# A hybrid attention layer on one core: first x block and warm-up, gates of the first up group, and the place of product 6 in the first output task

## The chip, the cores and the metric

The kernel runs on one core of a Trainium2 chip. The metric is the device time of one execution in microseconds (us); lower is better. The engines are PE (TensorE, matrix products), PEld (its weight loads), DVE (VectorE), ACT (ScalarE), POOL (GpSimd) and SP (SyncE); the last two mostly issue transfers (DMA) here.

## The reference

One layer over 512 tokens of width 2048, all in float32:

```
hn    = rmsnorm(x, norm_g)
proj  = hn @ w_in                      # q, k, v, gate of three branches, 4 forget logits, 3 merge gates
ya    = forgetting attention(q, k, v, f_logit)      # branch A, 4 heads of 128
yb    = chunked attention with relative bias        # branch B
yc    = stick-breaking attention                    # branch C
ys    = stack(ya, yb, yc) * silu(gate)
up    = einsum('bsnw,nwd->bsnd', ys, w_up)          # 512 -> 2048 for each branch
merged = sum over branches of sigmoid(merge gate) * up
out   = x + merged @ w_out                          # 2048 -> 2048
```

## The kernel before

**Products in two parts.** Every float32 operand of a large product is split in an upper part and the rest: ACT writes the upper part (`wh` for weights, line 366; `hi` for activations), DVE the lower part (`wl = raw - wh`, line 371; `lo`). Three matmuls (hi by wh, lo by wh, hi by wl) give one product. A weight block ("unit") is 256 rows by 512 columns: two pieces of 128 x 512. There are three `wh` buffers, two `wl` buffers and eight `raw` buffers, so the copies of a block begin when PE has left an older one.

**Order.** The instructions of PE, ACT and DVE stand in an order that a small planner in the kernel writes out: `Flow` keeps a clock per engine, tasks (Python generators) yield events, buffers or an engine with a cost, and the task that can start first is recorded next. The planner's costs and due times set only that order; on the chip each engine takes its list in order and waits by semaphores. Lists of `units` give the order of weight blocks, and `at(u, task)` starts a side task when PE's list comes to unit `u`.

**Stages.** (1) Until about 54 us: x is loaded transposed in 16 blocks of 128 x 512 (`loads`, on SP's queue), scaled by `norm_g` and split (`prep_x`), and multiplied with the columns of branch C's first head (`first_head`); x in its natural layout comes beside it for the norm (`norm_x`). PE begins with `WARM` small matmuls on an identity. (2) Until about 1014 us: the other heads and the merge gates. Behind the first group of gates, the products of 512 tokens by 2048 by two groups of 512 columns are done as Strassen tasks: seven products (named 5, 1, 6, 7, 4, 2, 3 in the order `PLAIN`) over half the tokens, each over four chunks `c` of the inner dimension, in place of eight. A merge gate's rows are stored to DRAM (`spill`). (3) 1014 to 1158 us: the up projection, in groups `g` of 512 output columns and, in each, the branches C, B, A. PE fills four `acc` banks, one for each block of 128 tokens (`tb`), by two units; for each bank DVE multiplies it with the sigmoid of the merge gate (`taken`, line 1251), which frees the bank. The gates are loaded back from DRAM by SP and go through ACT's sigmoid (`gates_of`, lines 1232 to 1236); `at(len(units) - 3 + tb // 2, ...)` starts these tasks. (4) From 1154 us: the output projection, two Strassen tasks (`out_task`). The merged rows of the last up group are turned on PE and combined into Strassen's operands (`m23`, `m2`, `m4`) by `merged_b` on DVE and ACT at the beginning of this stage.

In a Strassen task the weights of product 6 are those of product 5 plus those of product 1 of the same chunk: DVE adds them in the raw buffer (`sum_up`, line 574) once product 5's `wl` is made, and copies follow. The first output task is the one task with an order of its own: products 5, 1 and 6 for the chunks 0 and 1, then for the chunks 2 and 3, then `PLAIN`. So that three products are open at once, its product 6 has two banks of the other pool (`other = (6,)`, `att` in place of `acc`; each pool has four banks).

Of the kernel before, what the change touches and what calls it, by code (L numbers as in the profile page):

```python
# [8 lines left out]
F32 = mybir.dt.float32  # L9
F32R = mybir.dt.float32r  # L10
BF16 = mybir.dt.bfloat16
# [4 lines left out]
P = 128  # L16
S = 512
# [11 lines left out]
HS = S // 2  # L29
EPS = 1e-6  # L30
NEG = -1e30
WARM = 42
SCALE = HD ** -0.5
LA = 2

# [119 lines left out]
def act_us(n, x=1):  # L155
    return x * (0.075 + 0.00095 * n)


def dve_us(n, x=1):
    return x * (0.1 + 0.00105 * n)  # L160
# [3 lines left out]
def hybrid_kernel(  # L164
# [26 lines left out]
    def nm(s):  # L191
        uid[0] += 1
        return f"{s}_{uid[0]}"
# [6 lines left out]
    def t2(s, dt=F32):  # L200
        return tp.tile([P, S], dt, tag="t2", name=nm(s))
# [87 lines left out]

    nc.scalar.preload_act_table_set("natural_log_exp_and_others")  # L290
    small_in = cp.tile([P, consts.shape[1]], F32, name="small_in")
    nc.scalar.dma_start(small_in, consts)
    gn = small_in[:, 0:KT]
    gqk = small_in[:, KT:KT + 4]
    bfc = small_in[:, KT + 4:KT + 5]
    wf = small_in[:, KT + 5:].rearrange("p (k h) -> p k h", h=NH)

    epsc = cp.tile([P, 1], F32, name="epsc")
    nc.gpsimd.memset(epsc, EPS)
    nhepsc = cp.tile([P, 1], F32, name="nhepsc")  # L300
# [38 lines left out]
    def at(u, g, slack=5.0):  # L339
        side.setdefault(u, []).append((g, slack))  # L340
# [20 lines left out]
    def prep(u):  # L361
        n = u.shape[0] * S
        u.hi = wp.tile([P] + u.shape, F32R, tag="wh", name=nm("wh"), bufs=LA + 1)
        yield u.there
        yield ACT, act_us(n)
        nc.scalar.activation(u.hi, u.raw, AF.Copy)  # L366
        set_(u.ready_hi)
        yield wls, 1
        u.lo = wp.tile([P] + u.shape, F32R, tag="wl", name=nm("wl"), bufs=LA)
        yield DVE, dve_us(n)  # L370
        nc.vector.tensor_sub(u.lo, u.raw, f(u.hi))  # L371
        set_(u.ready)
        u.split_done()
# [39 lines left out]
    first_ps = att()  # L413
    atts.free.pop()
    nc.vector.memset(first_ps, 0.0)
    for _ in range(WARM):
        nc.tensor.matmul(first_ps[:, :P], identb, identb, start=True, stop=True)
    xps.free.clear()


# [5 lines left out]
    def prep_x(kt):  # L426

        due = (5.0 + 3.2 * kt,)
        yield x_in[kt]
        x = xraw[kt]  # L430
        if kt < 2:
            g = gn[:, kt:kt + 1]
            yield (ACT, act_us(S), *due)
            nc.scalar.activation(xs[kt].hi, two(x), AF.Copy, scale=g)
            set_(raw_hi[kt])
            yield (DVE, dve_us(S), *due)
            nc.vector.scalar_tensor_tensor(xs[kt].lo, two(x), g, f(xs[kt].hi), op0=ALU.mult, op1=ALU.subtract)
            set_(raw_ev[kt])
            yield (DVE, 0.5, due[0] + 5.0)
            nc.vector.tensor_scalar_mul(x, x, g)  # L440
            set_(scaled[kt])
            return
        if kt < 10:
            yield (DVE, 0.5, *due)
            nc.vector.tensor_scalar_mul(x, x, gn[:, kt:kt + 1])
        else:
            yield (ACT, 0.65, *due)
            nc.scalar.activation(x, x, AF.Copy, scale=gn[:, kt:kt + 1])
        set_(scaled[kt])
        yield from split(xs[kt].hi, xs[kt].lo, two(x), S, raw_ev[kt], due, raw_hi[kt])  # L450
# [777 lines left out]
    def gates_of(n, g, tb):  # L1228
        yield last_head.event("hl", 2)
        yield t2s, 1  # L1230
        t = sig[n, g, tb] = t2("sg")
        yield fetch(t, gl[n, g, tb], flow.now, 256)
        yield last_head.event("g")
        yield ACT, act_us(S) + 0.1
        nc.scalar.activation(t, t, AF.Sigmoid)  # L1235
        set_(sig_ev[n, g, tb])
# [111 lines left out]
    for g in (0, 2, 1, 3):  # L1348
        for b in range(NB):
            for tb in range(QB):  # L1350
                at(len(units) - 3 + tb // 2, lambda n=(C, B, A)[b], g=g, tb=tb: gates_of(n, g, tb))
            units.extend(up_units(g, b))
        for i in range(QB):
            at(len(units) - 1, lambda g=g, i=i: turned_m(g, i))
# [6 lines left out]
    def out_task(i):  # L1361
        where = dict(c11=(0, 0), c12=(2, 0), c21=(0, 1), c22=(2, 1))

        def place(name, tb):
            b, q = where[name]
            return b + tb, 2 * i + q

        def done(name, tb, c):
            yield ACT, 0.05
            nc.scalar.dma_start(out[place(name, tb)[0], place(name, tb)[1]], c)  # L1370
            stored(t2s, 1, 256)

        def rest(name, tb):
            return xn[place(name, tb)[0], place(name, tb)[1]]

        def src(m, half, c):
            return w_out[2 * i + m, CH * half + c]

        order, other = PLAIN, ()
        if i == 0:  # L1380
            order = [(p, c) for cs in ((0, 1), (2, 3)) for p in (5, 1, 6) for c in cs]
            order += PLAIN[3 * CH:]
            other = (6,)
        return Strassen(src, mops, done, order, other, rest).units

    for i in range(2):
# [3 lines left out]
    def loads():  # L1390
        def x(kt):
            yield t2s, 1
            xraw[kt] = t2("x")
            x_in[kt].t = fetch(xraw[kt], xT[kt], 0.0, 256).t

# [30 lines left out]
                spawn(u.after(), 0.0, flow.fin)  # L1426

    line[0] = 0.8
    flow.fin = 5.0
    spawn(loads(), 0.0, 0.0)  # L1430
    for kt in range(KT):
        spawn(prep_x(kt), 5.0)
# [62 lines left out]
```

## Time and profile before

| | |
|---|---|
| median of 3 runs | 1318.59 us (1318.33 to 1319.23) |
| profiled execution | 1318.87 us, span from first to last instruction 1317.2 us |
| busy share of the span | PE 99%, weight load 82%, DVE 78%, ACT 57%, POOL 7% |
| granted TensorE clock | 1.000 |
| transfers | 266.03 MB, 202 GB/s mean |

The span is what the profile's times run over, beginning at 0; the profiled execution's own time is 1.7 us more. Rows of a timeline give start and duration in us, the engine, the line, what is written and read, the number of instructions merged, and in brackets the time the engine was idle before and what released it. SPq, ACTq and POOL rows with DMA are the issue of a transfer, not the transfer.

### The profile page before, as it was taken

Reading aid. Unit: us, or ns where it says so; the run is one execution under the profiler, and the core shown is the slowest. Engines: PE = TensorE matmul, PEld = TensorE weight load, DVE = VectorE, ACT = ScalarE, POOL = GpSimd, SP = SyncE. Lnnn points to the kernel's source line nnn. Section 1 sums busy time; section 2 is a strip of 40 time slices with the busy share of each in tenths; the row PEclk is TensorE's granted clock in tenths of the full one; section 3 lists DMA queues with packets and bytes.
Section 4 is the critical chain, followed back from the end, with each engine's and each line's share of the span. In section 5 each row is a group of like instructions: output and inputs, shape, how many; then the busy total and the mean of one; then the engine's idle time right before and its main releaser. Section 6 shows DMA issues by size and latency. Waiting matters only on the chain.

```text
span 1317.2 us, 17191 instructions
## 1 busy us (share of the span) xinstructions
PE 1306.8 (99%) x6034; PEld 1078.7 (82%) x6034; DVE 1023.2 (78%) x1420; ACT 751.5 (57%) x1271; POOL 91.2 (7%) x115
## 2 busy tenths in 40 slices
PE   9999999999999999999999999999999999999998
PEld 7788888888888888888888888888887788878787
DVE  5877787887878777687776877778789668798667
ACT  7655464564557656566466654667568555454342
POOL 0000001110011100111011110110000000000110
PEclk9999999999999999999999999999999999999999
DMA  9755677866778757777577775777776656648883
GB/s 358 218 139 147 182 209 190 231 176 178 207 196 231 197 166 232 176 225 205 170 226 176 224 208 168 224 176 224 220 250 197 235 192 208 161 97 249 245 240 128
DMA packets 89063, 266.03 MB, mean 202 GB/s; under 512 B 11264, under 2 KB 11264, under 8 KB 88976
## 3 DMA queue, kind: packets, MB, share of 16 engines
q1 hardware_dynamic: 71552, 206.16, 46.5%
q0 software_dynamic: 14976, 54.53, 23.1%
q10 hardware_dynamic: 2448, 4.24, 0.8%
q8 instruction: 47, 0.77, 0.2%
q14 instruction: 40, 0.33, 0.1%
HBM read 245.19 MB, written 19.70 MB: 201 GB/s over the span
## 4 chain that ended last, share of the span: by engine, by line
PE 96%; DMA 2%; DVE 1%; ACT 1%; issue 0%; SPq 0%; ACTq 0%; POOLq 0%; DVEq 0%
PE acc L265 89%; DMA raw<-in_w_out 2%; PE att L801 1%; PE att L926 1%; PE att L260 1%; PE att L261 1%; PE att L262 1%; PE att L1016 1%; PE att L1015 1%; PE att L1285 1%; PE att L1014 1%; PE att L265 1%; ACT sg L1235 0%; DVE wl L371 0%; PE att L1118 0%; DMA x<-in_xT 0%
## 5 line engine op out<-in xcount | busy, mean ns | idle before, releaser
L371 DVE TENSOR_TENSOR wl<-raw,wh 128x1024 fp32r<-128x1024 f32 (+1 forms) x405 | 493.5, 1220 | 208.1 <-PE acc L265 116.1
L366 ACT ACTIVATE wh<-raw 128x1024 fp32r<-128x1024 f32 (+1 forms) x405 | 426.0, 1054 | 365.8 <-PE acc L265 276.3
L265 PE MATMUL acc<-wh,x 128*128 128x512 f32 x1664 | 429.8, 392 | 0.1
L265 PEld LDWEIGHTS acc<-wh,x 128*128 128x128 f32 x1664 | 308.7, 188 | 64.7 <-ACT t L246 0.9
L265 PE MATMUL acc<-wh,t 128*128 128x512 f32 x1056 | 272.6, 391 | 0.0
L265 PE MATMUL acc<-wl,x 128*128 128x512 f32 x832 | 229.8, 390 | 0.0
L265 PEld LDWEIGHTS acc<-wh,t 128*128 128x128 f32 x1056 | 196.7, 188 | 40.2
L265 PEld LDWEIGHTS acc<-wl,x 128*128 128x128 f32 x832 | 155.9, 188 | 33.1 <-DVE wl L371 0.4
L265 PE MATMUL acc<-wl,t 128*128 128x512 f32 x528 | 149.3, 390 | 0.0
L281 POOL DMA_DIRECT2D raw<-in_w_col x88 | 76.0, 864 | 877.5 <-ACT wh L366 195.3
L574 DVE TENSOR_TENSOR raw<-raw,raw 128x1024 f32<-128x1024 f32 x104 | 126.7, 1218 | 0.0
L265 PEld LDWEIGHTS acc<-wl,t 128*128 128x128 f32 x528 | 98.4, 188 | 19.6
L265 PE MATMUL acc<-wh,m 128*128 128x512 f32 x416 | 105.1, 390 | 1.9 <-ACT wh L366 1.9
L265 PE MATMUL acc<-wh,y 128*128 128x512 f32 x384 | 103.7, 391 | 1.3 <-DVE sg L1251 1.3
L265 PEld LDWEIGHTS acc<-wh,m 128*128 128x128 f32 x416 | 77.9, 188 | 18.8 <-ACT wh L366 2.7
L265 PEld LDWEIGHTS acc<-wh,y 128*128 128x128 f32 x384 | 71.7, 188 | 16.8 <-DVE sg L1251 2.2
L265 PE MATMUL acc<-wl,y 128*128 128x512 f32 x192 | 59.7, 391 | 0.0
L265 PE MATMUL acc<-wl,m 128*128 128x512 f32 x208 | 58.1, 390 | 0.1
L246 ACT ACTIVATE ah<-att 128x512 fp32r<-128x512 f32 (+3 forms) x48 | 21.0, 437 | 48.2 <-PE att L926 48.2
L265 PEld LDWEIGHTS acc<-wl,m 128*128 128x128 f32 x208 | 38.9, 188 | 8.5 <-DVE wl L371 0.5
L250 DVE TENSOR_TENSOR al<-att,ah 128x512 fp32r<-128x512 f32 (+3 forms) x48 | 23.5, 489 | 25.5 <-ACT ah L246 24.8
L265 PEld LDWEIGHTS acc<-wl,y 128*128 128x128 f32 x192 | 35.7, 188 | 7.2
(179 smaller groups left out, 1114.3 us busy)
## 6 DMA issues: line engine op xcount, KB each, us to landing
raw<-in_w_col SPq DMA_DIRECT2D x235, 512.0 KB, 4.6
raw<-in_w_col POOLq DMA_DIRECT2D x88, 512.0 KB, 7.9
raw<-in_w_out SPq DMA_DIRECT2D x40, 512.0 KB, 3.9
raw<-in_w_up SPq DMA_DIRECT2D x24, 512.0 KB, 3.6
sg<-gl SPq DMA_DIRECT2D x48, 256.0 KB, 4.6
raw<-in_w_out POOLq DMA_DIRECT2D x16, 512.0 KB, 6.2
gl<-u SPq DMA_DIRECT2D x22, 256.0 KB, 9.8
gl<-s SPq DMA_DIRECT2D x22, 256.0 KB, 5.2
```

The costliest lines, as they stand in the source:

```text
L246: nc.scalar.activation(hi, src, AF.Copy)
L250: nc.vector.tensor_sub(lo, src, f(hi))
L260: nc.tensor.matmul(ps, lh, rh, start=start, stop=False, skip_group_check=more)
L261: nc.tensor.matmul(ps, lh, rl, start=False, stop=False, skip_group_check=more)
L262: nc.tensor.matmul(ps, ll, rh, start=False, stop=stop, skip_group_check=more)
L265: nc.tensor.matmul(ps, w, x, start=start, stop=stop, skip_group_check=more)
L281: nc.gpsimd.dma_start(to, src, accum_op=ALU.add)
L366: nc.scalar.activation(u.hi, u.raw, AF.Copy)
L371: nc.vector.tensor_sub(u.lo, u.raw, f(u.hi))
L574: nc.vector.tensor_add(to.raw, to.raw, self.raw)
L801: nc.tensor.transpose(ps[:, blk(tb)], self.c[tb][:, blk(r)], identf)
L926: nc.tensor.transpose(ps[:, blk(i)], self.p[i][:, blk(j)], identf)
```

## The change

Three places.

1. The start. The first block of x is loaded on ACT's queue instead of SP's, and the constants (`small_in`) on SP's instead of ACT's. `WARM` is 36 instead of 42, and the warm-up works on a tile of ones that DVE writes first, into a bank of its own. The first weight block's `wh` is made on DVE. The blocks 2 and 3 of x are treated as the blocks 0 and 1 were: scaled inside the copies, and the plain scaled x, which only the forget logits and Strassen's operands need, later (due time 24 in place of 5 us after the block's). The planner's first times are adapted.
2. The up projection. The four gate tasks of the very first group (g = 0, branch C) are all started at `len(units) - 2`, in the order of the token blocks; all others stay at `- 3 + tb // 2`.
3. The first output task. Its order is products 5 and 1 for the chunks 0 and 1, products 5 and 1 for the chunks 2 and 3, then 6, 7, 4, 2, 3, and product 6 has `acc` banks.

```diff
-WARM = 42
+WARM = 36
...
-    nc.scalar.dma_start(small_in, consts)
+    nc.sync.dma_start(small_in, consts)
+    x_first = tp.tile([P, S], F32, tag="t2", name=nm("x"))
+    nc.scalar.dma_start(x_first, xT[0])
...
+    oneb = cp.tile([P, P], BF16, name="oneb")
+    nc.vector.memset(oneb, 1.0)
...
-        yield ACT, act_us(n)
-        nc.scalar.activation(u.hi, u.raw, AF.Copy)
+        if u is units[0]:
+            yield DVE, dve_us(n)
+            nc.vector.tensor_copy(u.hi, u.raw)
+        else:
+            yield ACT, act_us(n)
+            nc.scalar.activation(u.hi, u.raw, AF.Copy)
...
+    early_ps = att()
     for _ in range(WARM):
-        nc.tensor.matmul(first_ps[:, :P], identb, identb, start=True, stop=True)
+        nc.tensor.matmul(early_ps[:, :P], oneb, oneb, start=True, stop=True)
...
-        if kt < 2:
+        if kt < 4:
             g = gn[:, kt:kt + 1]
...
+            if kt == 0:
+                yield units[0].ready_hi
...
-            yield (DVE, 0.5, due[0] + 5.0)
+            yield (DVE, 0.5, 24.0)
             nc.vector.tensor_scalar_mul(x, x, g)
...
-                at(len(units) - 3 + tb // 2, lambda n=(C, B, A)[b], g=g, tb=tb: gates_of(n, g, tb))
+                at(len(units) - (3 - tb // 2 if g or b else 2), lambda n=(C, B, A)[b], g=g, tb=tb: gates_of(n, g, tb))
...
         if i == 0:
-            order = [(p, c) for cs in ((0, 1), (2, 3)) for p in (5, 1, 6) for c in cs]
-            order += PLAIN[3 * CH:]
-            other = (6,)
+            order = [(p, c) for cs in ((0, 1), (2, 3)) for p in (5, 1) for c in cs]
+            order += PLAIN[2 * CH:]
...
+            if kt == 0:
+                xraw[0], x_in[0].t = x_first, 3.6
+                return
...
-    flow.fin = 5.0
+    flow.fin = 4.0
```

What this does to the engines' lists, at three places. Names end in the buffers' numbers, which differ by a few between the two kernels; line numbers behind line 300 are 4 to 13 higher in the changed one.

The start, DVE, before. `x_27` and `x_29` are x's blocks 0 and 1, `raw_28` and `raw_30` the first two weight blocks:

```order
L322 COPY gq_101<-small_in_79 128x4
L324 TENSOR_SCALAR gq_101<-small_in_79 128x1 x2
L437 SCALAR_TENSOR_TENSOR x1_2_109<-x_27_181,small_in_79,x1_2_109 128x2x256
L440 TENSOR_SCALAR x_27_181<-x_27_181,small_in_79 128x512
L371 TENSOR_TENSOR wl_54_251<-raw_28_183,wh_51_245 128x512
L437 SCALAR_TENSOR_TENSOR x1_3_110<-x_29_185,small_in_79,x1_3_110 128x2x256
L371 TENSOR_TENSOR wl_60_266<-raw_30_187,wh_52_246 128x512
```

The same place on DVE in the changed kernel, where `x_1` and `x_30` are the blocks 0 and 1:

```order
L326 COPY gq_105<-small_in_79 128x4
L328 TENSOR_SCALAR gq_105<-small_in_79 128x1 x2
L371 CAST wh_52_242<-raw_29_180 128x512
L379 TENSOR_TENSOR wl_55_247<-raw_29_180,wh_52_242 128x512
L448 SCALAR_TENSOR_TENSOR x1_3_113<-x_1_81,small_in_79,x1_3_113 128x2x256
L448 SCALAR_TENSOR_TENSOR x1_4_114<-x_30_182,small_in_79,x1_4_114 128x2x256
L379 TENSOR_TENSOR wl_61_262<-raw_31_184,wh_53_243 128x512
```

The first weight block's upper and lower part stand ahead of x's first lower part, and the plain scaling of x's block 0 (line 440) has left this stretch.

The up projection, DVE, before. `acc_1740`, `acc_1744`, `acc_1746` and `acc_1750` are the banks of the token blocks 0 to 3 of branch C, group 0; `y` is the last head's output:

```order
L1023 TENSOR_TENSOR y_1719_8961<-y_1719_8961,att_1752_9116 128x512
L1251 TENSOR_TENSOR sg_1755_9123<-acc_1746_9087,sg_1755_9123 128x512
L250 TENSOR_TENSOR y_1761_9136<-y_1719_8961,y_1761_9136 128x2x256
L1251 TENSOR_TENSOR sg_1756_9125<-acc_1750_9101,sg_1756_9125 128x512
L371 TENSOR_TENSOR wl_1775_9208<-raw_1703_8888,wh_1764_9141 128x1024
L1251 TENSOR_TENSOR sg_1765_9142<-acc_1740_9055,sg_1765_9142 128x512
L1251 TENSOR_TENSOR sg_1770_9167<-acc_1744_9076,sg_1770_9167 128x512
```

The same place on DVE in the changed kernel; the banks are now `acc_1741`, `acc_1745`, `acc_1747` and `acc_1751`:

```order
L1262 TENSOR_TENSOR sg_1756_9120<-acc_1741_9052,sg_1756_9120 128x512
L1034 TENSOR_TENSOR y_1720_8958<-y_1720_8958,att_1753_9113 128x512
L1262 TENSOR_TENSOR sg_1757_9122<-acc_1745_9073,sg_1757_9122 128x512
L1262 TENSOR_TENSOR sg_1758_9124<-acc_1747_9084,sg_1758_9124 128x512
L250 TENSOR_TENSOR y_1764_9137<-y_1720_8958,y_1764_9137 128x2x256
L1262 TENSOR_TENSOR sg_1759_9126<-acc_1751_9098,sg_1759_9126 128x512
L379 TENSOR_TENSOR wl_1776_9207<-raw_1704_8885,wh_1766_9140 128x1024
```

The token blocks come in the order 0, 1, 2, 3 instead of 2, 3, 0, 1, the last head's `y` stands behind the first product, and the next weight's `wl` behind all four. On SP's and ACT's lists the loads and sigmoids of these gates trade places in the same way: 0 to 3 are the first four, where they were the ninth, tenth, first and second.

The first output task, PE, before, where product 1's second chunk ends (`acc_1988`, `acc_1989`):

```order
L265 MATMUL acc_1988_10352<-wl_1990_10354,m1_1824_9475 128x512
L265 MATMUL acc_1989_10353<-wl_1990_10354,m1_1824_9475 128x512
L265 MATMUL att_1998_10398<-wh_1987_10351,m23_1874_9740 128x512 x2
L265 MATMUL att_1999_10399<-wh_1987_10351,m23_1874_9740 128x512 x2
L265 MATMUL att_1998_10398<-wh_1987_10351,m23_1876_9746 128x512 x2
```

The same place on PE in the changed kernel:

```order
L265 MATMUL acc_1989_10349<-wl_1991_10351,m1_1825_9472 128x512
L265 MATMUL acc_1990_10350<-wl_1991_10351,m1_1825_9472 128x512
L265 MATMUL acc_1968_10270<-wh_1988_10348,m1_1933_10042 128x512 x2
L265 MATMUL acc_1969_10271<-wh_1988_10348,m1_1933_10042 128x512 x2
L265 MATMUL acc_1968_10270<-wh_1988_10348,m1_1935_10047 128x512 x2
```

Behind product 1's second chunk stands product 5's third (`acc_1968`, `acc_1969`) instead of product 6's first on `att` banks. DVE's list at this place, before (`raw_1912` and `raw_1925` are the weights of products 5 and 1 at chunk 1, `raw_1942` those of product 5 at chunk 2):

```order
L574 TENSOR_TENSOR raw_1912_9937<-raw_1912_9937,raw_1925_10016 128x1024
L250 TENSOR_TENSOR m2_1994_10372<-m_1972_10299,m2_1994_10372 128x2x256
L256 SCALAR_TENSOR_TENSOR mu_1981_10322<-mt_1985_10330,m_1984_10328 128x256
L371 TENSOR_TENSOR wl_2002_10407<-raw_1942_10085,wh_1997_10397 128x1024
L250 TENSOR_TENSOR m23_2000_10401<-mt_1980_10321,m23_2000_10401 128x2x256
L250 TENSOR_TENSOR m2_2001_10405<-m_1976_10308,m2_2001_10405 128x2x256
L371 TENSOR_TENSOR wl_2005_10427<-raw_1912_9937,wh_1995_10379 128x1024
```

And DVE's list in the changed kernel, up to product 5's last chunk (`raw_1951`; `raw_1943` is its third):

```order
L250 TENSOR_TENSOR m23_1993_10364<-mt_1978_10307,m23_1993_10364 128x2x256
L379 TENSOR_TENSOR wl_1997_10378<-raw_1943_10082,wh_1988_10348 128x1024
L256 SCALAR_TENSOR_TENSOR mu_1982_10319<-mt_1981_10318,m_1980_10316 128x256
L250 TENSOR_TENSOR m2_1995_10369<-m_1973_10296,m2_1995_10369 128x2x256
L585 TENSOR_TENSOR raw_1913_9934<-raw_1913_9934,raw_1926_10013 128x1024
L256 SCALAR_TENSOR_TENSOR mu_1982_10319<-mt_1986_10327,m_1985_10325 128x256
L379 TENSOR_TENSOR wl_2000_10399<-raw_1951_10132,wh_1996_10377 128x1024
```

Product 6's `wl` (`wl_2005` before) has left this stretch, and the sum of its weights stays in it.

## The prediction

> **What bounds the kernel now.** I read the page's busy shares and its chain first, then the waits of the matmul engine (PE), then the timeline where PE waits.
>
> ```profile
> PE 1306.8 (99%) x6034; PEld 1078.7 (82%) x6034; DVE 1023.2 (78%) x1420; ACT 751.5 (57%) x1271; POOL 91.2 (7%) x115
> PE 96%; DMA 2%; DVE 1%; ACT 1%; issue 0%; SPq 0%; ACTq 0%; POOLq 0%; DVEq 0%
> PE att L417 <- DVE identb L310: 1.9, 1, 1.9
> PE acc L265 <- ACT wh L366: 1.9, 2, 1.4
> PE acc L265 <- DVE sg L1251: 1.3, 1, 1.3
> PE att L265 <- DVE wl L371: 1.1, 1, 1.1
> ```
>
> PE is the bound: 96% of the chain. The four waits are total, times, longest, in us. The change removes no matrix product of the computation, so it can only win in the first 6.3 us, in the wait for the sg product, in the wait for wl on an att bank, and in the two waits for wh. A busy PE also hides a little: a matmul's modelled end overlaps the next, so I measure from start to start. Eight matmuls of 128x512 run in about 1.82 us, 0.227 each (22.85 to 26.50 below: 16 in 3.65).
>
> **The start.** The rows are start, duration, engine, line.
>
> ```profile
> 0.84 0.39 ACTq L292 DMA_DIRECT2D small_in<-in_consts  x1
> 1.25 0.90 SPq L277 DMA_DIRECT2D x<-in_xT  x2
> 1.93 4.31 PE L417 MATMUL att<-identb 128*128 128x128 bf16 x42 [1.93 <-DVE identb L310]
> 5.00 0.72 ACT L434 ACTIVATE x<-x,small_in 128x512 fp32r<-128x512 f32 x1 [2.90 <-DMA x<-in_xT]
> 5.62 0.61 ACT L366 ACTIVATE wh<-raw 128x512 fp32r<-128x512 f32 x1
> 6.29 2.11 PE L265 MATMUL acc<-wh,x 128*128 128x512 f32 x8
> ```
>
> ACT waits for x's first block until 5.00 and then does two copies in a row, x's and the weight's; PE starts at 6.29. Afterwards the x block is requested at about 0.84 (now 1.25) on ACT's queue, the constants go to the head of SP's queue and push the first weight block back by one issue (about 0.4), and everything behind on SP keeps its place, since one issue came and one left. The weight's copy goes to DVE beside ACT's (a one-input 128x512 copy; the nearest ACT row is 0.61). The same two blocks and the constants have to arrive, so the later of the two lands between 4.3 (0.4 earlier) and 4.95; then 0.72 on ACT and 0.6 on DVE run side by side, and PE starts between 5.1 and 5.7. DVE then makes wl before x's lower part, so PE may lose 0.2 to 0.5 after four matmuls. Head start by the second weight block: 0.4 to 0.7 us. The warm-up starts about 0.7 earlier, as it no longer waits for the identity, and has six matmuls fewer; it ends near 5.0.
>
> Does the head start live? The next rows say no.
>
> ```profile
> 12.00:40.00 28.00, 28.00 (x129) 22.20 (x131) 16.90 (x26) 25.31 (x57) 0.00 (x0) 1.00 1.04 396
> ```
>
> ```profile
> 21.63 1.06 ACT L366 ACTIVATE wh<-raw 128x1024 fp32r<-128x1024 f32 x1 [0.22 <-DMA raw<-in_w_col]
> 22.85 3.82 PE L265 MATMUL acc<-wh,x 128*128 128x512 f32 x16
> ...
> 32.29 1.06 ACT L366 ACTIVATE wh<-raw 128x1024 fp32r<-128x1024 f32 x1
> 33.26 0.70 ACT L448 ACTIVATE x<-x,small_in 128x512 f32<-128x512 f32 x1
> 34.00 0.63 ACT L246 ACTIVATE x<-x 128x512 fp32r<-128x512 f32 x1
> 34.68 1.45 PEld L265 LDWEIGHTS acc<-wh,x 128*128 128x128 f32 x7 [0.28 <-ACT x L246]
> ```
>
> The first row is a window: PE, weight load, DVE, ACT, POOL busy, clock, DMA share, GB/s. From 12 to 40 us the transfers are full (share 1.04, 396 GB/s). At 21.63 ACT waits for a weight block to land; its copy ends at 22.69, and PE uses it at 22.85. So PE reaches that block only 0.16 before it is bound by the transfers, and at 34.68 its weight load waits for ACT, whose queue has run without a pause since the block of 32.29. The order of these ACT rows does not change. A PE 0.4 to 0.7 earlier waits at 22.7 and again at 34.7: what is left of the head start is 0.0. Bounds: a gain of 0.7 if all landings come that much earlier, a loss of 0.4 if the constants ahead on SP push all behind them by an issue.
>
> A row that leaves room for such a gain is the window of the first 6.2 us:
>
> ```profile
> 0.00:6.20 6.20, 4.27 (x42) 4.13 (x42) 1.86 (x7) 2.49 (x4) 1.39 (x11) 1.00 0.70 209
> ```
>
> 209 GB/s over 6.2 us are 1.30 MB; at 396 the time after the first 1.9 us would carry 1.70 MB. By this row a second queue could save up to 1.0 us. [...] I take 0.
>
> The other edits at the start: the blocks x2 and x3 are scaled inside the copies, as x0 and x1 are now, and the plain scaling for the later forget product moves behind. The number of DVE passes over them stays; ACT loses one. Cover: ACT and DVE are ahead of PE up to the third weight block. Without it each late 128x512 pass would cost some 0.7, and that too is lost in the wait of 22.7. I take 0.
>
> **The first up group.** PE fills four acc banks for branch C, and DVE's product with the gate frees each.
>
> ```profile
> 1025.10 2.20 ACT L1235 ACTIVATE sg<-sg 128x512 f32<-128x512 f32 x4
> 1026.57 0.69 DVE L1251 TENSOR_TENSOR sg<-acc,sg 128x512 f32<-128x512 f32 x1 [0.81 <-PE acc L265]
> 1027.66 1.07 PE L265 MATMUL acc<-wh,y 128*128 128x512 f32 x4
> 1029.20 1.19 PE L265 MATMUL acc<-wh,y 128*128 128x512 f32 x4
> 1029.71 3.22 ACT L1235 ACTIVATE sg<-sg 128x512 f32<-128x512 f32 x6
> 1030.23 0.63 PE L265 MATMUL acc<-wl,y 128*128 128x512 f32 x2
> 1031.40 1.29 DVE L1251 TENSOR_TENSOR sg<-acc,sg 128x512 f32<-128x512 f32 x2 [1.12 <-ACT sg L1235]
> 1032.14 1.20 PE L265 MATMUL acc<-wh,y 128*128 128x512 f32 x4 [1.29 <-DVE sg L1251]
> ```
>
> Today the gates of the token blocks 2 and 3 are loaded first and those of 0 and 1 ninth and tenth, so the third sigmoid that PE's banks need is in the batch of 1029.71 and ends near 1031.4; PE, which would go on at 1030.23 + 0.45 = 1030.68, starts at 1032.14: 1.46 lost. At 1029.20 it lost 0.18 (1028.56 + 0.46 = 1029.02), and after each stop the first four matmuls take 0.12 more. Sum: 1.9.
>
> Afterwards the four gates are the first four sigmoids, one each 0.52 from 1025.10, done at 1025.7 to 1027.3; the number of loads and sigmoids does not change, nor their place on SP (the same nine slots hold other tiles). DVE's order becomes: product 0, the head's y, products 1 and 2, y's lower part, product 3. With 0.69 each from 1025.75: the products end at 1026.5, 1027.8, 1028.4 and 1029.8. PE needs the banks every six matmuls, 1.36: at 1027.66, 1029.02, 1030.38 and 1031.74. Each is free 1.1 to 2 us before. The head's y is now 0.7 later; nothing needs it before branch A's second unit, 16 us on. Gain 1.9. Between 0 (the sigmoids late by over 1.2 us plus the stall) and 1.9 I take 1.9, since the first four sigmoids ran back to back in the row of 1025.10, their loads landed.
>
> **The first output task.** Product 6 waits for a weight sum, its copy and wl on a full DVE.
>
> ```profile
> 1163.62 0.42 DVE L256 SCALAR_TENSOR_TENSOR mt<-mt,m 128x256 f32<-128x256 f32 x1
> ...
> 1169.57 1.22 DVE L371 TENSOR_TENSOR wl<-raw,wh 128x1024 fp32r<-128x1024 f32 x1
> 1169.99 2.07 PE L265 MATMUL att<-wh,m 128*128 128x512 f32 x8
> 1171.91 1.22 DVE L371 TENSOR_TENSOR wl<-raw,wh 128x1024 fp32r<-128x1024 f32 x1
> 1173.18 1.20 PE L265 MATMUL att<-wl,m 128*128 128x512 f32 x4 [1.12 <-DVE wl L371]
> 1173.98 0.69 DVE L250 TENSOR_TENSOR m<-m,m 128x512 fp32r<-128x512 f32 x1
> 1174.58 0.42 DVE L250 TENSOR_TENSOR m<-mu,m 128x256 fp32r<-128x256 f32 x1
> ```
>
> The eight matmuls of 1169.99 should have led on at 1171.81; PE goes on at 1173.18: 1.37, and 0.12 after it: 1.5. The wl at 1169.57 was for product 5's third chunk, ahead of the one that PE stood at (1171.91).
>
> Afterwards PE does product 5 and 1 over all four chunks (21.8 us) before product 6. DVE is still full; the tightest place is wl for product 5's last chunk. From the shared row at 1163.62 DVE now has four operations of 128x256 (0.42), two of 128x512 (0.69) and three of 128x1024 (1.22, wl and sum alike) before it; starts follow 0.09 before the end of the last (1173.98 + 0.69 against 1174.58). That is 4 x 0.33 + 2 x 0.60 + 3 x 1.13 = 5.9, so this wl runs from 1169.5 to 1170.8. PE, unstopped, starts that chunk at 1169.99 and needs wl after four matmuls, at 1170.9. It fits by 0.1; a miss costs the miss. Later wl have over 1 us, and product 6's sums are 10 us ahead. The weights are no transfer more: the same eight blocks lie in the eight raw buffers. Product 6 moves from att banks to acc banks, freed by ACT's copies of product 5 some 5 us before. Gain 1.4 to 1.5; bounds 0 and 1.5.
>
> What is late next is the second output task, where the two waits for wh hang on weight blocks that are added up by POOL's transfers:
>
> ```profile
> 1222.27 9.44 DMA raw<-in_w_out
> 1232.26 11.08 DMA raw<-in_w_out
> ```
>
> These start when DVE and ACT free a raw buffer, which follows PE product by product, so the whole of it moves ahead with PE; this stall I leave as it is, and PE's waits for wh stay 1.9.
>
> **Sum.** 0.0 + 1.9 + 1.4 = 3.3 us. The profiled execution took 1318.87 (span 1317.2); the median of the runs is 1318.59, 0.3 below. So 1315.3 in runs.
>
> **Rivals.**
> A. The head start lives: all landings come 0.4 to 0.7 earlier because two queues fill the engines sooner. For it speaks 209 GB/s at the start, against it the share of 0.70 and the full stream behind. 1314.7.
> B. The stall in the output task comes back: wl of product 5 or the added blocks of the second task, not PE, set the pace. For it the margin of 0.1, and 9 to 11 us per added block; against it that the starts of these blocks follow PE. Then only the up group's 1.9 is left: 1316.7.
> C. The clock. The warm-up's matmuls ran at half rate until 5.64:
>
> ```profile
> 1.92:5.64 3.72, 3.71 (x36) 3.72 (x37) 0.00 (x0) 1.00 0.99 288
> 5.64:6.24 0.60, 0.59 (x9) 0.42 (x7) 0.00 (x0) 1.00 0.99 372
> ```
>
> 37 weight loads took 3.72 us, 0.10 each, and seven then 0.42, 0.06 each. Now 36 are given and PE then idles for up to 0.7. If the fast rate came only after the real matmuls had run a while, each would cost 0.2 more (0.227 doubled, about). It starts 0.5 ahead, so 3.7 us at half rate cost 1.4: 1316.7. It decides against the change from about 8 us of half rate on (3.3 + 0.5 over 0.5), that is if the rate stayed low up to the third weight block; then 1319 to 1321. Against it: the new warm-up still lasts 3.7 us, and PE's stop of 1.29 at 1032 did not lower the rate (1.20 for four). [...]
>
> **Numbers.** A measurement of this kernel can tell about 0.2%, 2.6 us. The forecast (both stalls gone, start even) has 0.60; A 0.12 (here all faster); B 0.16; C and any other loss at the start 0.12, a third of it slower than before. The forecast with its own spread of 0.5 lies over 2.6 nine times in ten: faster 0.69 (0.54 + 0.12 + 0.03), same 0.27, slower 0.04. The range runs from A with an early start (1314.1) to past B (1317.2).
>
> **What would show it.** Right: no wait of PE for sg near 1030, none for wl near 1172, the first real matmul before 5.8, the weight block of 22.7 waited for, and PE at 35 where it was. Wrong: PE at 35 us earlier or later by over 0.3; a new wait for wl in product 5; longer waits for wh near 1240; half-rate matmuls after 5 us.

## The result: 3.2 us less, and where they come from

| | before | changed |
|---|---|---|
| median (12 executions each) | 1318.76 us (1317.73 to 1320.72) | 1315.53 us (1314.95 to 1317.40) |
| profiled execution | 1318.87 us, span 1317.2 | 1315.29 us, span 1313.6 |

The ratio is 0.9977, with a 95% interval of 0.9969 to 0.9986: faster by 0.23%, and the interval excludes no change. The forecast was 1315.3 us.

The busy shares, from the page of the changed kernel's profile:

```profile
PE 1305.8 (99%) x6028; PEld 1078.7 (82%) x6028; DVE 1023.2 (78%) x1422; ACT 752.1 (57%) x1270; POOL 91.3 (7%) x115
```

They are those of before; what changed is in PE's waits (total, times, longest, in us):

```profile
PE acc L265 <- ACT wh L374: 2.2, 1, 2.2
PE att L426 <- DVE oneb L301: 1.1, 1, 1.1
PE acc L265 <- DVE wh L371: 0.2, 1, 0.2
```

The waits for `sg` (1.3) and for `wl` on an `att` bank (1.1) are gone. The wait for `wh` is there still, but as one wait of 2.2 where there were two with 1.4 the longest. From start to start of the matmuls, the last one comes 3.63 us earlier, and this divides so: up group 1.92, first output task 1.43, start 0.31, second output task -0.04.

The start, from the timeline of the changed kernel (start, duration, engine, line; in brackets the idle time before and what ended it):

```profile
0.84 0.39 ACTq L294 DMA_DIRECT2D x<-in_xT  x1
1.13 3.96 PE L426 MATMUL att<-oneb 128*128 128x128 bf16 x36 [1.13 <-DVE oneb L301]
4.09 0.72 ACT L443 ACTIVATE x<-x,small_in 128x512 fp32r<-128x512 f32 x1 [2.00 <-DMA x<-in_xT]
4.68 0.43 DVE L371 CAST wh<-raw 128x512 fp32r<-128x512 f32 x1 [0.76 <-DMA raw<-in_w_col]
5.26 2.49 PE L265 MATMUL acc<-wh,x 128*128 128x512 f32 x8 [0.17 <-DVE wh L371]
5.75 0.75 DVE L448 SCALAR_TENSOR_TENSOR x<-x,small_in,x 128x512 fp32r<-128x512 f32 x1
```

PE begins at 5.26 instead of 6.29, with a stop of 0.41 behind four matmuls, as x's lower part (5.75) stands behind the weight's. The copy on DVE takes 0.43, against 0.61 on ACT. At the block of 22.85 PE is 0.55 ahead; then:

```profile
22.30 3.79 PE L265 MATMUL acc<-wh,x 128*128 128x512 f32 x16
33.18 4.24 PE L265 MATMUL acc<-wh,x 128*128 128x512 f32 x16
41.00 1.20 PE L265 MATMUL acc<-wh,x 128*128 128x512 f32 x4
```

The row of 33.18 takes 4.24 where 16 matmuls take 3.79: a stop. At 41 us, 0.29 us of the head start is left.

The first up group, on DVE and PE:

```profile
1025.45 0.69 DVE L1262 TENSOR_TENSOR sg<-acc,sg 128x512 f32<-128x512 f32 x1 [1.65 <-ACT sg L1246]
1026.65 1.28 DVE L1262 TENSOR_TENSOR sg<-acc,sg 128x512 f32<-128x512 f32 x2
1028.45 0.68 DVE L1262 TENSOR_TENSOR sg<-acc,sg 128x512 f32<-128x512 f32 x1
1028.70 1.07 PE L265 MATMUL acc<-wh,y 128*128 128x512 f32 x4
1030.06 1.07 PE L265 MATMUL acc<-wh,y 128*128 128x512 f32 x4
1031.42 1.07 PE L265 MATMUL acc<-wh,y 128*128 128x512 f32 x4
```

The four products are done at 1026.1, 1027.3, 1027.9 and 1029.1; PE takes a new bank every 1.36 us, and none of its rows has a bracket, that is, a wait.

The first output task, at its tightest place:

```profile
1167.34 1.22 DVE L379 TENSOR_TENSOR wl<-raw,wh 128x1024 fp32r<-128x1024 f32 x1
1168.61 0.30 PEld L265 LDWEIGHTS acc<-wl,m 128*128 128x128 f32 x2 [0.21 <-DVE wl L379]
1168.66 0.67 PE L265 MATMUL acc<-wl,m 128*128 128x512 f32 x2
```

`wl` of product 5's last chunk is ready at 1168.56, and the first matmul that needs it starts at 1168.66. It and the next one take 0.06 longer than elsewhere (to 1169.17): the only trace of the old stop of 1.37.

The second output task, before, and then changed:

```profile
1240.10 2.12 PE L265 MATMUL acc<-wh,m 128*128 128x512 f32 x8 [0.43 <-ACT wh L366]
1244.55 1.19 PE L265 MATMUL acc<-wh,m 128*128 128x512 f32 x4 [1.44 <-ACT wh L366]
```

```profile
1228.49 0.86 POOL L281 DMA_DIRECT2D raw<-in_w_out  x1 [5.29 <-DMA raw<-in_w_out]
1234.00 1.06 ACT L374 ACTIVATE wh<-raw 128x1024 fp32r<-128x1024 f32 x1 [2.52 <-DMA raw<-in_w_out]
1239.79 2.96 ACT L374 ACTIVATE wh<-raw 128x1024 fp32r<-128x1024 f32 x3 [4.73 <-DMA raw<-in_w_out]
1240.90 1.20 PE L265 MATMUL acc<-wh,m 128*128 128x512 f32 x4 [2.18 <-ACT wh L374]
```

The third added block is now in time (its copy of 1234.00 is done 0.8 us before PE comes to it at 1235.84); the fourth, requested at 1228.49, lands 11.3 us later. What follows the fourth block moved by 3.65 us, about as its request did (3.77 us, from 1232.26 to 1228.49). In sum, from start to start, the stops are 2.80 us, 2.75 before.

### The profile page after: what moved, and what is told of

Same layout as the page of the kernel before. It is cut to its first block, busy times and chain, and to the rows that moved or that the text cites. A ratio compares the mean times of both kernels' runs of the same rounds, so it can differ in the third digit from the quotient of the medians.

```text
span 1313.6 us, 17186 instructions
## 1 busy us (share of the span) xinstructions
PE 1305.8 (99%) x6028; PEld 1078.7 (82%) x6028; DVE 1023.2 (78%) x1422; ACT 752.1 (57%) x1270; POOL 91.3 (7%) x115
## 4 chain that ended last, share of the span: by engine, by line
PE 95%; DMA 3%; ACT 1%; DVE 0%; issue 0%; SPq 0%; ACTq 0%; POOLq 0%; DVEq 0%
PE acc L265 89%; DMA raw<-in_w_out 2%; PE att L812 1%; PE att L937 1%; DMA raw<-in_w_col 1%; DMA x<-in_xT 1%; PE att L260 1%; PE att L1027 1%; PE att L1026 1%; PE att L261 1%; PE att L262 1%; PE att L1025 1%; PE att L1296 1%; PE att L1129 0%; ACT wh L374 0%; ACT xn L487 0%
## 5 line engine op out<-in xcount | busy, mean ns | idle before, releaser
L265 PE MATMUL acc<-wh,m 128*128 128x512 f32 x448 | 113.1, 389 | 2.2 <-ACT wh L374 2.2
L265 PEld LDWEIGHTS acc<-wh,m 128*128 128x128 f32 x448 | 84.0, 188 | 20.1 <-ACT wh L374 2.6
L265 PE MATMUL acc<-wl,m 128*128 128x512 f32 x224 | 62.6, 390 | 0.1
L265 PEld LDWEIGHTS acc<-wl,m 128*128 128x128 f32 x224 | 41.8, 188 | 9.2 <-DVE wl L379 0.7
```

What stands on the lines that cost most here:

```text
L265: nc.tensor.matmul(ps, w, x, start=start, stop=stop, skip_group_check=more)
```

## Experiments

### Each of the three parts alone

The kernel before, with one part of the change each: the gate line; the order of the first output task; all edits of the start. The code below shows the first two, shortened.

```diff
(gates alone)
-                at(len(units) - 3 + tb // 2, lambda ...
+                at(len(units) - (3 - tb // 2 if g or b else 2), lambda ...
(first output task alone)
-            order = [... for p in (5, 1, 6) for c in cs]
-            order += PLAIN[3 * CH:]
-            other = (6,)
+            order = [... for p in (5, 1) for c in cs]
+            order += PLAIN[2 * CH:]
```

Gates: 

> The kernel before with the new order of the first up group's gates alone. By the prediction's term: 1.9 us less than before (about 1316.7), no wait of PE for sg near 1030, and every later place of PE about 1.85 us earlier. Rival (the stall comes back further on, since the weights or the other gates are late instead): within 0.3 us of before, with a new stop of PE between 1032 and 1050. What can tell: the two stops of PE at 1029.2 and 1032.1, and PE's place at the start of the output stage.

First output task: 

> The kernel before with the new order of the first output task alone. By the prediction's term: 1.4 to 1.5 us less (about 1317.2), no wait for wl near 1172, and the second task's stops near 1240 as long in sum as before (2.75 us from start to start) but possibly in another division, as the fourth added block moves ahead with PE. Rival (the added blocks of the second task, not PE, set the pace): the stops near 1240 grow by as much as was won, and the time is that of before.

Start: 

> The kernel before with the edits of the start alone. By the prediction's term: 0.0, PE at 41 us where it was in the kernel before (41.29). By the trace of the whole change: 0.3 us less, PE at 41.0, because the weight blocks of 21 to 32 us land 0.6 to 0.7 earlier (the slowest of the 16 DMA engines is 1.6 us behind the first, not 2.3). If that lag depends on where an instruction fetch of 16 KB falls and not on the edits, PE's place at 41 may come out anywhere between 40.5 and 41.5. Rival A (the head start lives whole): 0.6 less. Rival C (clock): the first real matmuls of 512 columns at over 0.4 us each, and 1 us or more lost.

| kernel | median | ratio to before (median 1319.17) |
|---|---|---|
| gates alone | 1317.09 | 0.9985 (0.9976 to 0.9994) |
| first output task alone | 1316.90 | 0.9986 (0.9977 to 0.9994) |
| start alone | 1319.76 | 1.0003 (0.9994 to 1.0011) |

The gains are 2.1, 2.3 and -0.6 us: the two stalls make the gain, and the start none that can be told from zero. Each interval reaches some 1.2 us to either side, so the sizes come from the traces: there PE comes 1.92 us earlier by the gates alone and 1.43 by the output task alone, as in the whole change. PE's waits with the gates alone:

```profile
PE att L417 <- DVE identb L310: 1.9, 1, 1.9
PE acc L265 <- ACT wh L366: 1.6, 2, 1.4
PE att L265 <- DVE wl L371: 1.1, 1, 1.1
```

and with the output task alone:

```profile
PE att L417 <- DVE identb L310: 1.9, 1, 1.9
PE acc L265 <- ACT wh L366: 1.7, 2, 1.4
PE acc L265 <- DVE sg L1251: 1.3, 1, 1.3
```

Each part removes its own wait and leaves the other's, and no new wait comes. Both rivals (a stop further on; the added blocks give the gain back) fall: the stops near 1240 are 2.46 and 2.55 us here, each summed from start to start.

### Does the head start live?

In the profile of the start alone, PE takes the block of 22.85 at 21.97, 0.9 us ahead, and is at 41.35 in place of 41.29, 0.06 behind the kernel before. The same is seen in a repeat of the changed kernel (below), of which these are rows of ACT and PE:

```profile
21.94 3.79 PE L265 MATMUL acc<-wh,x 128*128 128x512 f32 x16
26.71 1.06 ACT L374 ACTIVATE wh<-raw 128x1024 fp32r<-128x1024 f32 x1 [0.21 <-DMA raw<-in_w_col]
27.82 3.94 PE L265 MATMUL acc<-wh,x 128*128 128x512 f32 x16 [0.28 <-ACT wh L374]
33.45 4.31 PE L265 MATMUL acc<-wh,x 128*128 128x512 f32 x16
41.33 0.96 PE L265 MATMUL acc<-wh,x 128*128 128x512 f32 x3
```

ACT waits for the block to land (26.71), PE for ACT (27.82), and the row of 33.45 holds another stop (4.31 for 3.79). So the 0.9 us are lost to the transfers and to the copies behind them, as forecast, though at 27.8 and 34.5 and not at 22.7. How much is eaten differs from execution to execution, with the landings. PE's place at 41 us in the profiles of all kernels:

| start | first real matmul | PE at 41 us |
|---|---|---|
| old (before, gates alone, output task alone, by turns with old start) | 6.29, 6.15, 6.17, 6.35 | 41.29, 40.81, 40.88, 41.28 |
| new (changed, repeat, start alone, pairs, by turns, staggered, filled) | 5.26, 5.06, 5.04, 5.17, 5.13, 5.05, 5.10 | 41.00, 41.33, 41.35, 41.68, 41.20, 40.64, 41.04 |
| new, one warm-up matmul (alone, with pairs) | 5.09, 5.18 | 41.40, 42.16 |

The means of the first two rows are 41.07 and 41.18: 1.1 us of earlier start, and nothing of it left that can be seen beside a spread of 1 us. The 0.29 of the first profile lies within that spread.

The records of landings in the traces tell why. A block has 16 partial landings there, and ACT copies it once the last is in: in the kernel before the last part landed at 21.53, and the copy began at 21.63. Of the block that PE takes at 22.85 in the kernel before, the first part landed at 18.93 to 19.27 us in the four profiles with the old start and at 18.84 to 19.39 in the nine with the new one: the stream did not come earlier. The last part came 0.9 to 2.7 us behind the first (2.29 before, 1.60 changed, 0.89 in the repeat), and this lag moves the copy. In the start alone it grows from 1.1 to 2.2 us when a packet of 16 KB on the instruction queue takes 1.04 us, from 19.54 on, and in the repeat from 0.9 to 2.0 at such a packet of 19.91; in the changed kernel's first profile (20.26) only from 1.6 to 1.7. That these packets make the lag is a guess from the times; no run tests it.

The other side was tried too: a start that is worse for PE (`WARM = 1`).

> The changed kernel with one warm-up matmul in place of 36. Its first real matmuls then run at half rate for 3.4 to 6.8 us, each 0.43 in place of 0.227 us, and PE comes 1.7 to 3.4 us later to the weight block of 22.3 us. Theory: of the head start of 0.55 at that block and the stop of 0.37 at 34.4 us, up to 0.9 us is taken from the delay, so PE is 0.8 to 2.5 us later at 41 us and in time. Rival (the transfers, not PE, set the pace up to 35 us, whatever PE does): PE at 41 us unmoved and the time that of the changed kernel.

Measured: 1314.57 us (1313.92 to 1315.33). The first matmuls did run at half rate:

```profile
5.09 3.69 PE L265 MATMUL acc<-wh,x 128*128 128x512 f32 x8 [3.68 <-DVE wh L371]
23.16 3.79 PE L265 MATMUL acc<-wh,x 128*128 128x512 f32 x16
34.04 3.79 PE L265 MATMUL acc<-wh,x 128*128 128x512 f32 x16
41.40 0.96 PE L265 MATMUL acc<-wh,x 128*128 128x512 f32 x3
```

Eight take 3.5 us instead of 1.8, 0.44 each for 0.227. The 3.4 to 6.8 us expected were an estimate, once and twice the 3.41 us for which the clock was halved in the start alone (below); it was 3.5 us or more here, and 4.9 with the order in pairs. PE is 1.2 us later than in the repeat at the second row (23.16 against 21.94), meets no stop from there on, and is at 41 us only 0.07 later. So my theory (0.8 to 2.5 us lost) was too dear and the rival nearer: until 35 us the landings set the pace, and the 36 warm-up matmuls gain nothing that the times show. This kernel is 0.5 us below the repeat. In its profile the stop in the second output task is 1.69 us, as the fourth block landed after 10.3 us instead of 11.3, and the mean clock is 1.000 in all five executions. Where the half rate lasted until 10.1 us (with the order in pairs, below), PE was 0.5 later at 41 than in that kernel's warm execution, and later than the 41.7 expected, but the time was only 0.1 us longer.

### The clock behind the one stop

The start alone came out 0.6 us slower, though PE stood at 1032 where it stood before. Its profile shows a cause, in three windows (columns: length; PE, weight load, DVE, ACT, POOL busy with their counts; granted clock; DMA share; GB/s):

```profile
1241.78:1245.19 3.41, 1.28 (x6) 0.77 (x5) 0.31 (x1) 1.39 (x2) 0.00 (x0) 1.00 0.67 254
1245.19:1248.60 3.41, 3.41 (x9) 2.62 (x9) 3.19 (x3) 2.15 (x3) 0.00 (x0) 0.50 0.00 0
1248.60:1252.01 3.41, 3.41 (x16) 2.75 (x16) 2.36 (x2) 2.14 (x3) 0.00 (x0) 1.00 0.50 154
```

A stop of 2.3 us before the fourth added block, and for 3.41 us behind it the granted clock is 0.50: nine matmuls where 16 run otherwise. I call this a fall of the clock. Six of the 11 executions of the start alone have a mean clock of 0.998, and seven of the 27 of the kernel before beside them; the medians of the others are 1318.79 and 1318.96. To see whether the changed kernel has this, it was run again.

> The changed kernel once more, for the times of single executions beside those of the next kernels. Theory of the clock: the one stop of PE near 1239 (2.3 us) lies within a window of 3.41 us in some executions, and the clock is then halved for the window after it, which costs 1.7 us; so about a quarter of the executions should lie near 1317 and the others near 1315.4. Rival: the stop has no such effect, and the times lie evenly about one median.

Median 1315.05 us. Its 23 executions (12 and 11) fall in two groups: 14 from 1314.61 to 1315.58, nine from 1316.35 to 1317.40, none between; the groups' medians are 1315.08 and 1316.59. The profiled one is of the upper group and shows the same:

```profile
1237.69:1241.11 3.42, 1.52 (x8) 0.94 (x7) 0.16 (x1) 1.25 (x2) 0.00 (x0) 1.00 0.89 345
1241.11:1244.52 3.41, 3.41 (x9) 2.64 (x10) 3.34 (x3) 2.30 (x3) 0.00 (x0) 0.50 0.01 5
```

The first profile of the changed kernel, with a longer stop, does not:

```profile
1237.09:1240.51 3.42, 1.63 (x8) 1.01 (x6) 0.00 (x0) 0.72 (x1) 0.00 (x0) 1.00 0.98 374
1240.51:1243.92 3.41, 2.96 (x12) 2.12 (x13) 3.04 (x3) 2.84 (x4) 0.00 (x0) 1.00 0.02 8
```

The windows are not chosen freely: in each of four traces the clock's changes lie a whole multiple of 3.4133 us apart. In the kernel before it rose at 5.715 us and fell at 1316.433, 384.0 windows later; in the first profile of the changed kernel at 4.880 and 1312.184, 383.0 windows; in the start alone it rose at 6.149 us and fell at 1245.188, 363.0 windows later; in the repeat at 5.481 and 1241.10, 362.0 windows. The windows of the profile without a fall lie on its own grid, counted from its first rise at 4.880. Windows with PE busy for 1.28 and 1.52 us were followed by the half rate, the one with 1.63 was not. Two more windows lie at the end of the program, where PE runs out of work, of the start alone and of the repeat:

```profile
1313.46:1316.87 3.41, 1.38 (x7) 0.80 (x5) 1.37 (x2) 0.00 (x0) 0.00 (x0) 1.00 0.31 123
1309.37:1312.79 3.42, 1.49 (x7) 0.91 (x5) 1.38 (x2) 0.00 (x0) 0.00 (x0) 1.00 0.29 111
```

Behind the first the granted clock is 0.50, behind the second still 1.00. By these five windows a limit would lie near 1.4 to 1.5 us, an estimate, and the busy times do not give it more closely: in the repeat alone, the fall came behind 1.52 and not behind the smaller 1.49. The trial was to fill the stop with work that nobody needs (code shortened):

```diff
+    filled = units[-7 * CH + CH - 1]          # second task, product 5, last chunk
+    def fill(u):
+        yield atts, 1
+        ps = att()
+        for _ in range(26):
+            nc.tensor.matmul(ps[:, :P], oneb, oneb, start=True, stop=True)
+        give(atts)
+        yield from plain_mms(u)
+    filled.mms = fill
```

> The changed kernel, with 26 matmuls of 128x128 on the tile of ones (results unused) ahead of the unit at which PE stops near 1239. They take 26 x 0.056 = 1.5 us of a stop of 2.0 to 2.3 us, so they delay nothing. Theory: the halved clock near 1241 comes from a window of 3.41 us with too little work for PE (0.37 and 0.29 of it where the clock fell, 0.40 where it did not); with the stop filled no window falls below 0.6, no execution has the loss of 1.6 us, and all lie near 1315.1, where the changed kernel has two groups, near 1315.1 and 1316.6. Rival: the two groups come from something else; they stay.

Measured: 1315.07 us, all five from 1315.06 to 1315.63.

```profile
1238.60 1.62 PE L1408 MATMUL att<-oneb 128*128 128x128 bf16 x26
1240.66 1.20 PE L266 MATMUL acc<-wh,m 128*128 128x512 f32 x4 [0.44 <-ACT wh L375]
```

```profile
1237.94:1241.35 3.41, 2.97 (x33) 2.40 (x32) 0.71 (x1) 1.80 (x2) 0.00 (x0) 1.00 0.74 293
```

The matmuls delay nothing and no execution lies in the upper group. With nine of 23 there otherwise, five in a row outside it would come by chance about once in twelve times (0.61 to the fifth power is 0.08), so the five times alone are weak. The mean clock of each execution says more. One window at half rate takes 0.0013 off it (half of 3.41 us in 1314), and the end of the program took at most 0.0007 in these profiles: 1.000 leaves no room for a fall, 0.998 is more than the end alone took, and 0.999 can be either. All seven executions of the changed kernel with 0.998 lie in its upper group, and none with 1.000 does. All five of the filled kernel have 1.000, and so have 22 of the 25 of the kernels below, whose stop is 1.5 us or less. With this I hold it for shown of this kernel that an emptied window brings the fall, and the fall the upper group.

The kernel before has such executions too: ten of 51 have 0.998, with a median of 1320.34 against 1319.00 for the others. Whether the change made them more frequent is not settled. Nor is every late execution one of them: one each of the gates alone (1319.15), the output task alone (1319.00) and the staggered order below (1315.51) lies some 2 us above its median at a mean clock of 1.000, and no trace shows why.

### The stop itself

The second output task begins with four added blocks in a row. First, its order was made that of the first task:

```diff
-        if i == 0:
+        if True:
             order = [(p, c) for cs in ((0, 1), (2, 3)) for p in (5, 1) for c in cs]
```

> The changed kernel, with the second output task in the same order as the first (products 5 and 1 for the chunks 0 and 1, then for 2 and 3). Theory: the last large stop of PE, 2.8 us near 1239, comes from four added blocks in a row, each two transfers one behind the other; with a block of product 1 between them PE needs one only every second block (10.9 us), so the stop goes and the time is about 1312.7. Rival: the added blocks are begun when a raw buffer comes free, and product 1's blocks take buffers too, so that each added block starts later than now; the stop only moves, or the weight sums on DVE make PE wait for wl: 1315 to 1316.

Then by turns, with the new and the old start:

```diff
+        else:
+            order = [(p, c) for c in range(CH) for p in (5, 1)] + PLAIN[2 * CH:]
```

> The changed kernel, with products 5 and 1 of the second output task by turns, chunk by chunk (5,0 1,0 5,1 1,1 and so on). Theory: of the 2.8 us stop, the order in pairs left 1.2 us, as its last two added blocks were requested at 1233.2 and 1234.4, one behind the other; by turns they are needed 10.9 us apart, and no stop is left: 2.8 us less than the changed kernel, 1312.7, and no execution with a halved clock. Rival: raw buffers, not the order, set when the added blocks start; the stop stays at 1.2 us or more: 1313.7 or above.

> The kernel before's start, with the changed order of gates, the changed first output task, and products 5 and 1 of the second output task by turns. Theory (start 0.0): within 0.5 us of the same kernel with the changed start. By a gain of 0.3 from the start, as the first profile seemed to show: 0.3 more. Rival A (the head start lives): 0.6 more.

Then staggered, and the pairs with a cold start:

```diff
+            order = [(5, 0), (5, 1), (1, 0), (5, 2), (1, 1), (5, 3), (1, 2), (1, 3)] + PLAIN[2 * CH:]
```

> The changed kernel, with the second output task's order 5,0 5,1 1,0 5,2 1,1 5,3 1,2 1,3. Theory: added blocks are needed every second unit, as by turns, but the weight sums on DVE come two units later, so that neither a landing (1.2 us left in the order in pairs) nor wl on DVE (1.5 us left by turns) stops PE: 2.5 us less than the quick executions of the changed kernel, 1312.5. Rival: one of the two remains: 1313.7 or more.

> The order in pairs in the second output task and one warm-up matmul in place of 36. Theory (the warm-up is worth nothing, as PE waits for transfers until 35 us): the time of the order in pairs with the warm-up, 1313.5 +- 0.5, PE at 41 us between 41.0 and 41.7. Rival (the single kernel with one warm-up matmul was quick for another reason, and the cold start costs): 1 us more.

| second task | median | ratio to before | stops left there |
|---|---|---|---|
| pairs | 1313.73 | 0.9957 (0.9945 to 0.9970) | 1.2 us, wh |
| by turns | 1314.20 | 0.9961 (0.9949 to 0.9974) | 1.5 us, wl |
| by turns, old start | 1313.86 | 0.9958 (0.9945 to 0.9972) | 1.5 us, wl |
| staggered | 1313.40 | 0.9957 (0.9943 to 0.9970) | 1.2 us, wh |
| pairs, one warm-up matmul | 1313.83 | 0.9957 (0.9945 to 0.9969) | 0.8 us, wh |

By the medians they lie 0.9 to 1.7 us below the repeat of the changed kernel; the first two and the staggered order were expected 2.5 to 2.8 below. My expectation held an error: a block is 12 matmuls, 2.72 us, so every second block is 5.4 us and not 10.9, while an added block takes some 10 us with two of them under way. The orders halve the shortage, they don't end it. By turns, the wait for `wh` is gone, and DVE, which has sums and lower parts to make in the same stretch, takes its place:

```profile
1248.47 0.73 PE L265 MATMUL acc<-wl,m 128*128 128x512 f32 x2 [0.47 <-DVE wl L379]
1251.96 0.73 PE L265 MATMUL acc<-wl,m 128*128 128x512 f32 x2 [0.46 <-DVE wl L379]
```

Staggered, DVE's waits are gone, and one landing is late:

```profile
1239.33 2.14 PE L265 MATMUL acc<-wh,m 128*128 128x512 f32 x8 [0.94 <-ACT wh L374]
```

So in each version one of the two rivals named beforehand keeps about half of the stop. The staggered order is the quickest kernel of these, though its interval does not part it from the pairs. By turns, the old and the new start differ by 0.34 us, the old one ahead: once more nothing for the head start.

## Why the prediction was right, and where not

**Up group, 1.9: right.** 1.92 in the trace, 2.1 by the times of this part alone. The products came in the order told; put on the changed kernel's clock (0.31 earlier at the first sigmoid, 1024.79), the forecast ends are 1026.2, 1027.5, 1028.1 and 1029.5, and they were 1026.1, 1027.3, 1027.9 and 1029.1.

**First output task, 1.4 to 1.5: right, by the margin that was told.** It was 1.43 in the trace. The forecast had `wl` of the last chunk from 1169.5 to 1170.8; less the 2.2 us by which PE was ahead by then, 1167.3 to 1168.6, and it ran from 1167.34 to 1168.56. The margin of 0.1 was 0.06 too small for PE's weight load, and that cost 0.06. The count of DVE's operations up to the needed one decided this, not DVE's mean share.

**Start, 0.0: right in amount, wrong in place.** First matmul at 5.26 (forecast 5.1 to 5.7), 0.64 ahead at the second weight block (0.4 to 0.7), a stop of 0.41 for x's lower part (0.2 to 0.5). But PE did not wait at 22.7; the head start went at 34.4 in the first profile, and at 27.8 and 34.5 in the repeat. What failed is the step that took one execution's landing at 21.63 for the bound. The same block of the same start, in the kernel with the new gates alone:

```profile
20.70 1.06 ACT L366 ACTIVATE wh<-raw 128x1024 fp32r<-128x1024 f32 x1 [0.23 <-DMA raw<-in_w_col]
22.57 3.79 PE L265 MATMUL acc<-wh,x 128*128 128x512 f32 x16
```

It landed 0.9 us earlier, and PE took it 0.8 after the copy. A place in one trace bounds a stream only to within the spread of its landings. Nor did the two copies on ACT alone hold PE back: in the three other profiles with the old start they were done by 5.7 us, and the first matmul (6.15 to 6.35) came behind the last of the 42 warm-up matmuls. ACT began x's first copy at 5.00 in the profile before, at 4.27 to 4.39 in these three, and at 3.87 to 4.09 in all with the new start. That a second queue saves the stream nothing was my estimate; what the runs showed is that, beside those three, the first block gained some 0.4 us, the issue time saved (0.84 in place of 1.25), and the stream behind it nothing.

**Second output task, "stays 1.9": the sum right, its cost to the clock missed.** The whole moved ahead with PE, as told, and cost 2.80 for 2.75 from start to start. But I carried it as a number and did not ask how it lies: the stops of 2.1 and 2.3 us left PE busy for 1.52 and 1.28 of the 3.41 us of a window, and the half rate followed. Rival C looked for the half rate at the start only, where it costs nothing that the times show (the cold start), and not behind the longest stop, where the nine of 23 executions are 1.5 us longer and move the median by about 0.4 (1315.50 over all 23, 1315.08 over the 14). The kernel before has such executions too, so part of this falls out of the difference. In the profile of the result, 0.31 us come from a start that on the mean gives nothing. So the nearness of 1315.5 to 1315.3 owes something to chance.

**Rivals.** A (head start lives) falls with the start alone and the old start by turns; B (the pace is set by `wl` or added blocks) falls with the output task alone. Of C (the clock at the start), the sign did come in some executions: with 36 warm-up matmuls the half rate lasted until 3.85 to 6.87 us, by the records of the clock and the matmuls' durations (the column of the clock shows 1.00 ahead of its first change; in the kernel before, the warm-up's matmuls follow each other every 0.107 us up to it, every 0.056 behind it). The latest of these, the staggered order, ran its first real matmuls at half rate from 5.05 to 6.87 and was still the first of all at 41 us (40.64), so the loss that C feared did not follow.

## What to carry to other kernels

A stall is worth its start-to-start length only if the next engine in line has slack at that place: count its operations up to the one that is needed, since a margin of 0.1 us decided over 1.4 here. Do not spend edits on the first microseconds while a full stream of transfers bounds what follows; look where PE stands once the stream lets go, over several executions (here 1.1 us of earlier start left nothing at 41 us). And ask of a stop of PE that remains not only how long it is but how it lies: one of some 2 us within one window of the clock cost 1.5 us more than its length here.

## What was unexpected of the hardware

The clock of TensorE fell to half behind stops of 2.1 and 2.3 us, shorter than the 3.413 us of which the times between its changes are whole multiples. PE was busy for 0.38 and 0.44 of the window by the profile's rows (1.28 and 1.52 of 3.41 us) in the two cases with a fall, 0.44 and 0.48 (1.49 and 1.63) in the nearest ones without, and the half rate lasted exactly one window, 3.413 us, worth 1.7 us of work. Between the clock's rise and its fall lay 362.0 and 363.0 such windows in these two cases. PE did not have to stand still for a whole window: in both it was at work for over a third of the one ahead of the fall.

The fourth added block, two transfers one behind the other into the same buffer, landed 10.2 to 11.3 us after the request of its second one in the eight profiles with four added blocks in a row, so a wait that ends with it differs by 1 us between executions.
